# Weight sums of three pairs made by adding transfers, the root sent through DRAM, and four leading units kept in SBUF, at the entrance to the second ffn

## The chip, the cores and the metric

The kernel runs on one core of one Trainium2 chip. The metric is the device time of one execution in microseconds (us), less is better. A comparison is made from the medians of several runs; the profile is one further execution, with its own time.

Five engines matter: TensorE (PE for its matmuls, PEld for its weight loads), VectorE (DVE), ScalarE (ACT), GpSimd (POOL), and SyncE (SP), which here only issues transfers. POOL issues transfers too, on a queue of its own; those that add into their destination all go there.

## The reference

One decoder layer for 512 prompt tokens and 8 decode tokens (520 columns in all), float32, model width 1024, ffn width 2816:

```python
x = x + 0.5 * rmsnorm(swiglu(rmsnorm(x, ffn1_pre_g), ffn1_w_gate, ffn1_w_up, ffn1_w_down), ffn1_post_g)
m, ... = token_mixer(rmsnorm(x, mix_pre_g), ...)
x = x + rmsnorm(m, mix_post_g)
x = x + 0.5 * rmsnorm(swiglu(rmsnorm(x, ffn2_pre_g), ffn2_w_gate, ffn2_w_up, ffn2_w_down), ffn2_post_g)
```

with `swiglu(x) = (silu(x @ w_gate) * (x @ w_up)) @ w_down`. The token mixer runs a retention and a gated delta-rule branch side by side and ends in `y = sigmoid(gate_r) * (o_r @ w_ret_branch) + sigmoid(gate_g) * (o_g @ w_gdn_branch)`, then `y @ w_out`. The change lies between the end of that sum `y` and the first third of the second ffn.

## The kernel before, in words

**Layout.** Activations lie transposed: 8 tiles of 128 features by 520 tokens, in two halves of 260 columns (`HALVES`). A float32 product is made of three matmuls in the fast float32 format (`passes`, lines 414 to 416): high part of the weight by high part of the activation, high by low, low by high. So each weight tile is split first: ACT makes the high part (line 355, or 373 for half tiles) and DVE the low part (356, 374).

**Order of the work.** One Python program writes the instructions of all engines in one order. `tick` (line 223) is its clock: the loops that emit matmuls call it once per step of six matmuls, and it runs the side tasks (generators) that are due. A task that says `yield 4` goes on four steps later. Each engine carries out its own instructions strictly in the order written; an engine whose next instruction waits holds up all that are written behind it. The same holds for the transfers queued on SP and on POOL. `LATER` shifts single tasks by hand.

**Weights.** `unit_list` is the list of weight units in order of use. SP loads the raw unit of 512 KB into a ring of two buffers (`load_to`, lines 276 and 287), so a load waits until the split of the unit two before it is done. Splits run some units ahead (`prefetch`, line 312), unless `hold` is set, or, for pair units, `hold_sums`.

**Pairs.** In the second ffn the hidden tiles 0 to 3 are plain: 4 gate and 4 up products of 8 steps each. From tile 4 on, gate and up of a tile form a "pair": a 2 by 2 block product made with seven half-size products instead of eight (`SEVEN`, line 143; `product7`, line 843; tile name `sv` in the profile). With the blocks a11, a12 (gate) and a21, a22 (up), the seven weights are a11, a12, a22 and the sums s1 = a21 + a22, s3 = a11 + a21, s2 = a11 + a21 + a22 (with a sign) and s4 = a12 + a11 + a21 + a22. `begin_pair` (291) loads a first term of s1 and s3 and the whole a22 from SP; `add_sums` (304) then issues two adding transfers from POOL (line 307), each 256 KB. s2 and s4 are made on DVE when their turn comes (369 and 377). The token sides of the seven products are made by `token_factors` (801) on ACT and DVE; their high and low parts on 824 and 825.

**The end of the mixer.** `mixer` (1151) runs eight products of the first branch, then eight of the second (lines 1250 to 1259). `branch` (1262) evacuates each: for the second branch DVE forms gate times product (1281), POOL adds the first branch's part (1282), and three steps later ACT and DVE split the sum (1287, 1288) for the product with w_out, which `down` makes: five outputs one by one, and the last three with the first halves of all ahead of the second halves (`staged`). At its third output `down` loads x back (743, eight loads of 260 KB on SP). When a half is complete, `post` (629) takes the sum of squares over partitions by matmul (477), the inverse root on POOL (471, from `root`), spreads it over partitions by matmul (483, from `spread`) and adds the scaled output to x on POOL (647).

**The entrance to the second ffn.** `first_units` (765) runs the four leading units (gate and up of tiles 0 and 1) first over the first half of the tokens, then over the second. The first halves' four results are copied by ACT into two SBUF tiles "early" (792); the second halves' stay in their PSUM banks, of which there are eight. Meanwhile `pre_rms` (539) sums the squares of x, and `inverse_rms` (555) takes the root; four steps later it spreads each half by matmuls into a PSUM bank of its own and copies it to SBUF, one half by ACT (573), one by DVE (571). `hidden` (882) needs these two halves r[0], r[1] before it can use the leading units' results (889, 896). `token_factors` begins when the root instruction has been issued (`rooted`), and first issues the loads of the first two pairs (`begin_pairs`, 797). `hold_sums` is set from the start of `post` until r is there. `keep` (1072) stores x to DRAM once r is there.

Of the kernel before, what the change touches and what calls it, by code (L numbers as in the profile page):

```python
# [15 lines left out]
P = 128  # L16
# [14 lines left out]
HALVES = ((0, HC), (HC, HC))  # L31
BRANCH_HALVES = ((0, 256), (256, TOK - 256))
PIECES, PW = 3, -(-HC // 3)
PIECE_AT = [i * (HC - PW) // (PIECES - 1) for i in range(PIECES)]
KH = KD // 2
PAD = CONV_W - 1
TURN = 48
# [5 lines left out]
PLAIN = {1: 3, 2: 4}  # L43
SPLIT_H = (8, 21)
LEAD = 3
GATE_COLS = 72


# [122 lines left out]
class Kernel:  # L171
    def __init__(self, ctx, tc, a):
        self.tc, self.nc, self.a = tc, tc.nc, a
        nc = tc.nc
        pool = lambda name, **kw: ctx.enter_context(tc.tile_pool(name=name, **kw))
        self.cpool = pool("const", bufs=1)
        self.big = pool("big", bufs=SLOTS)
        self.raw = pool("raw", bufs=RAW_BUFS)
        self.whl = pool("whl", bufs=SPLIT_BUFS)
        self.wk = pool("wk", bufs=2)  # L180
        self.sm = pool("small", bufs=8)
        self.ps = pool("ps", bufs=8, space=PSUM)
        self.dram = pool("scratch", bufs=1, space=DRAM)
        self.n = 0
        self.unit_list = units()
        self.group, g, pairs = [], -1, {}
        for u in self.unit_list:
            if u[0] not in ("seven", "down7"):
                g += 1
                self.group.append(g)  # L190
                continue
            if u[0:3] not in pairs:
                g += 1
                pairs[u[0:3]] = g
            self.group.append(pairs[u[0:3]])
        self.group.append(g + 1)
        self.first_of = {}
        for j, g in enumerate(self.group):
            self.first_of.setdefault(g, j)
        self.loaded, self.begun = {}, {}  # L200
        self.split_done = {}
        self.raw_next = self.split_next = self.use_next = 0
        self.slots_used = 0
        self.freed = []
        self.sums_due = []
        self.hold_sums, self.pairs_upto = False, 0
        self.rooted = False
        self.ahead = 0
        self.tasks = []
        self.spawned = {}  # L210
        self.hold = False
        self.leads = 0
        self.now = 0
# [53 lines left out]
    def load_to(self, j):  # L267

        nc, a = self.nc, self.a
        while self.raw_next < min(self.group[min(j, len(self.unit_list))] + RAW_BUFS, self.group[-1]):  # L270
            u = self.unit_list[self.first_of[self.raw_next]]
            if u[0] == "seven":
                w, m = a[f"gu{u[1]}"], u[2]
                s1, s3, a22 = self.begun.pop((u[1], m), None) or self.begin_pair(u[1], m)
                t = self.raw.tile([P, KD, P], F32, tag="raw", name=self.name("raw"))
                nc.sync.dma_start(out=t, in_=w[2 * m])
                t = [t[:, 0:KH], s3, None, a22, t[:, KH:KD], s1, None]
            elif u[0] == "down7":
                t = []
                for d in (u[2], u[2] + 1):  # L280
                    raw = self.raw.tile([P, KD, P], F32, tag="raw", name=self.name("raw"))
                    nc.sync.dma_start(out=raw, in_=a[f"dn{u[1]}"][d, :, 0:KD, :])
                    t += [raw[:, 0:KH], raw[:, KH:KD]]
            else:
                kind, m, k0, k1 = u
                t = self.raw.tile([P, k1 - k0, P], F32, tag="raw", name=self.name("raw"))
                nc.sync.dma_start(out=t, in_=a[kind][m, :, k0:k1, :])
            self.loaded[self.raw_next] = t
            self.raw_next += 1
# [68 lines left out]
    def split_seven(self, j):  # L358

        nc = self.nc  # L360
        self.load_to(j)
        i = self.unit_list[j][3]
        t = self.loaded[self.group[j]]
        if i:
            self.add_sums(self.group[j])
        s2, s4 = 2, 6
        if i == s2:
            t[s2] = self.slot("s2", (P, KH, P))
            nc.vector.scalar_tensor_tensor(out=t[s2], in0=t[5], scalar=-1.0, in1=t[0], op0=ALU.mult, op1=ALU.subtract)  # L369
        w = self.whl.tile([P, 2, KH, P], F32R, tag="w", name=self.name("w7"))  # L370
        self.split_done[j] = (w[:, 0], w[:, 1])
        self.started(j)
        nc.scalar.copy(w[:, 0], t[i])  # L373
        nc.vector.tensor_tensor(w[:, 1], t[i], w[:, 0].bitcast(F32), ALU.subtract)  # L374
        if i == 4:
            t[s4] = self.slot("s4", (P, KH, P))
            nc.vector.tensor_tensor(t[s4], t[4], t[s2], ALU.subtract)

# [176 lines left out]
    def inverse_rms(self, acc, r, plus, held=False):  # L555
        nc = self.nc
        ps = self.bank("ss")
        self.sums(ps, acc, 2 * PIECES)
        m, s = self.root(ps, 2 * PIECES, 1.0 / D)
        if plus is not None:  # L560
            nc.vector.tensor_scalar(plus[0:PW], m[0:PW], EPS, None, ALU.mult)
        self.rooted = True
        self.hold = held
        if held:
            self.hold_sums = False
        yield 4
        out = self.wk.tile([P, TOK], F32, tag="rb", name=self.name("rb"), bufs=1)
        for hf, (c0, n) in enumerate(HALVES):
            pb = self.spread(s[:, hf * PIECES : (hf + 1) * PIECES])
            if hf:  # L570
                nc.vector.tensor_copy(out[:, c0 : c0 + n], pb)
            else:
                nc.scalar.copy(out[:, c0 : c0 + n], pb)
                if held:
                    yield 1
        for hf, (c0, n) in enumerate(HALVES):
            r[hf] = out[:, c0 : c0 + n]
        self.hold_sums = False

    def post_last(self, pairs, acc, sq, hf, plus):  # L580
# [184 lines left out]
    def first_units(self, xs, name, groups):  # L765
# [1 line left out]

        n = sum(len(g) for g in groups)
        ws, banks = [None] * n, [[None, None] for _ in range(n)]
        early = [self.slot("early") for _ in range(n // 2)]  # L770
        for hf, (c0, cols) in enumerate(HALVES):
            for group in groups:
                ps = {}
# [11 lines left out]
                for j in group:  # L785
                    banks[j][hf] = ps[j]
                    if hf:
                        self.release()
                    else:
                        rows = slice(0, ws[j][0].shape[2])  # L790
                        banks[j][0] = early[j // 2][rows, j % 2 * HC : j % 2 * HC + cols]
                        self.nc.scalar.copy(banks[j][0], ps[j][rows])
                if hf:
                    self.leads += 1
        return banks
# [1 line left out]
    def begin_pairs(self, f):  # L797
        for m in range(PLAIN[f], PLAIN[f] + 2):
            self.begun[f, m] = self.begin_pair(f, m, 24 if f == 1 and m > PLAIN[f] else SUM_LAG)

    def token_factors(self, xs, r, gcol, F, f):

        nc = self.nc
        while len(xs[1]) < KD or f == 2 and not self.rooted:
            yield 0

        if f == 2:
            self.begin_pairs(f)
        tt, stt = nc.vector.tensor_tensor, nc.vector.scalar_tensor_tensor
        for k in range(KH):  # L810
            x11, x12, x21, x22 = (self.x_of(z, hf) for z in (k, k + KH) for hf in range(2))
# [6 lines left out]
            nc.scalar.activation(ta[:, 0], d[:, 1], AF.Copy, scale=g1)  # L818
            stt(out=tb[:, 0], in0=x11, scalar=g1, in1=ta[:, 1], op0=ALU.mult, op1=ALU.subtract)
            stt(out=tb[:, 1], in0=x21, scalar=g2, in1=tb[:, 0], op0=ALU.mult, op1=ALU.subtract)  # L820
            yield 1
            for t, names in ((ta, ("T1", "T3")), (tb, ("T2", "T4"))):
                hi, lo = self.slot("th", (P, 2, HC), F32R), self.slot("tl", (P, 2, HC), F32R)
# [327 lines left out]
    def mixer(self, xs, r, plus_next, x_from):  # L1151
# [95 lines left out]
        for g in (GR, GG):  # L1247
            for m in range(KD):
                project(g, m)
        for out, g in ((RG, GR), (GZ, GG)):  # L1250
            for m in range(0, KD, 2):
                while out not in done:
                    self.tick()
                ox = [[self.ohl[out, h, hf] for h in range(H)] for hf in range(2)]
                hi, lo = self.next_unit()
                for z in range(2):
                    ks = slice(z * H, (z + 1) * H)
                    ps = self.product([((hi[:, ks, :], lo[:, ks, :]), range(H))], ox, "br", z, BRANCH_HALVES)
                    self.spawn(self.branch(g, m + z, gate.pop((g, m + z)), ps, part, yx))
        return self.down(yx, (8,), self.vec[:, V_MPOST : V_MPOST + 8], V_G2PRE, 3, None, plus_next, x_from)  # L1260

    def branch(self, g, m, gate, ps, part, yx):
# [15 lines left out]
        for hf, (c0, n) in enumerate(BRANCH_HALVES):  # L1278
            cs = slice(c0, c0 + n)
            ts.append(whole[:, cs])  # L1280
            nc.vector.scalar_tensor_tensor(out=ts[hf], in0=gate[:, cs], scalar=1.0, in1=ps[hf], op0=ALU.add, op1=ALU.mult)
            nc.gpsimd.tensor_tensor(ts[hf], ts[hf], part[m][:, cs], ALU.add)  # L1282
        yield 3
        for hf, (c0, n) in enumerate(BRANCH_HALVES):
            cs = slice(c0, c0 + n)
            t = ts[hf]
# [749 lines left out]
```

## Time and profile before

| | us |
|---|---|
| three runs: median (lowest to highest) | 1190.89 (1189.58 to 1191.94) |
| the profiled execution, its own time | 1189.49 |
| its span, first to last instruction | 1187.7 |
| TensorE matmul busy in it | 1172.0 |
| VectorE busy | 907.3 |
| ScalarE busy | 602.6 |
| GpSimd busy | 265.2 |
| end of the last product of the second branch, start of the product with w_out | 768.25 |
| the root of `inverse_rms` on POOL | 844.78 |
| the first pair products ("sv") | about 870 |

Places below are given in us from the start of the span. A row of the timeline has start, duration, engine, line, operation, output<-inputs, shapes and count, and in brackets how long the engine had been idle and what ended that. A row of the groups has the count, the busy time and mean duration in ns, and the idle time before them. A row of the waits has the total, the number of waits and the longest. A row of the windows has, for each engine, busy time and count, then the granted clock, the mean busy share of the 16 DMA engines, and GB/s. A row of the DMA queues has packets, MB, and the time the packets took as a share of 16 engines over the window; a row of the DMA issues has the count, the KB of each, and the median time from issue to landing.

### The profile page before, as it was taken

The numbers are of one execution on the slowest core, as the hardware profiler recorded it, in microseconds if no ns is written. First come the engines' busy times: TensorE is split into PE (matmuls) and PEld (weight loads), VectorE is DVE, ScalarE is ACT, GpSimd is POOL, SyncE is SP. The second block draws the span as 40 slices with busy tenths as digits, with TensorE's granted clock in tenths as the row PEclk, the third lists the DMA queues.
The fourth block names the chain that finished last, engine by engine and source line by source line (L and its number), as shares of the span: only waits on it lengthen the run. The fifth ranks groups of instructions, "written<-read, shape, count | busy, mean of one in ns | idle before, by whom it ended". The sixth has DMA issues, their size and how long they took to land. (4 is left out here: it accounts for less than half of the span.)

```text
span 1187.7 us, 25427 instructions
## 1 busy us (share of the span) xinstructions
PE 1172.0 (99%) x9831; PEld 1161.0 (98%) x9831; DVE 907.3 (76%) x1935; ACT 602.6 (51%) x1378; POOL 265.2 (22%) x477
## 2 busy tenths in 40 slices
PE   9999999999999999999999999999999999999998
PEld 8999999999999999999999999999999999999997
DVE  7988888777558788887677777746888888867555
ACT  7656666544336456313354774335555666644331
POOL 1111111000005248755551101404211111000000
PEclk9999999999999999999999999999999999999999
DMA  8777775233342533322367653242677777332334
GB/s 264 186 196 188 183 176 142 70 114 87 109 174 62 179 92 107 105 83 74 111 193 224 225 197 125 76 157 89 178 217 191 185 187 183 103 97 67 98 113 148
DMA packets 79178, 170.90 MB, mean 144 GB/s; under 512 B 17040, under 2 KB 18992, under 8 KB 79056
## 3 DMA queue, kind: packets, MB, share of 16 engines
q1 hardware_dynamic: 66768, 144.98, 38.1%
q0 software_dynamic: 12288, 24.29, 11.9%
q8 instruction: 77, 1.26, 0.4%
q14 instruction: 45, 0.37, 0.1%
HBM read 157.37 MB, written 11.86 MB: 142 GB/s over the span
## 5 line engine op out<-in xcount | busy, mean ns | idle before, releaser
L414 PE MATMUL p<-xhl,whi 128*128 128x260 f32 (+1 forms) x784 | 231.1, 295 | 0.0
L415 PE MATMUL p<-xhl,whi 128*128 128x260 f32 (+1 forms) x784 | 221.3, 282 | 0.1
L416 PE MATMUL p<-xhl,wlo 128*128 128x260 f32 (+1 forms) x784 | 221.2, 282 | 0.0
L356 DVE TENSOR_TENSOR wlo<-raw,whi 128x1024 fp32r<-128x1024 f32 (+2 forms) x111 | 132.9, 1202 | 50.1 <-ACT whi L355 48.4
L414 PE MATMUL sv<-th,w 128*128 128x260 f32 x592 | 167.6, 283 | 1.8 <-ACT q L912 1.8
L415 PE MATMUL sv<-tl,w 128*128 128x260 f32 x592 | 167.1, 282 | 0.0
L416 PE MATMUL sv<-th,w 128*128 128x260 f32 x592 | 167.1, 282 | 0.0
L415 PEld LDWEIGHTS p<-xhl,whi 128*128 128x128 f32 (+1 forms) x784 | 147.2, 188 | 0.7 <-DVE xhl L518 0.7
L414 PEld LDWEIGHTS p<-xhl,whi 128*128 128x128 f32 (+1 forms) x784 | 146.9, 187 | 0.9 <-DVE qk L1562 0.2
L416 PEld LDWEIGHTS p<-xhl,wlo 128*128 128x128 f32 (+1 forms) x784 | 147.0, 187 | 0.0
L307 POOL DMA_DIRECT2D s<-gu_in x74 | 65.0, 954 | 308.4 <-DMA s<-gu_in 156.1
L374 DVE TENSOR_TENSOR w<-s,w 128x512 fp32r<-128x512 f32 x148 | 101.6, 689 | 37.6 <-ACT w L373 36.7
L414 PE MATMUL dn<-hh,whi 128*128 128x260 f32 x448 | 127.0, 283 | 0.0
L415 PE MATMUL dn<-hl,whi 128*128 128x260 f32 x448 | 126.7, 283 | 0.0
L416 PE MATMUL dn<-hh,wlo 128*128 128x260 f32 x448 | 126.6, 283 | 0.0
L355 ACT CAST whi<-raw 128x1024 fp32r<-128x1024 f32 (+2 forms) x111 | 111.0, 1008 | 30.7 <-DMA raw<-dn_in 16.2
L414 PEld LDWEIGHTS sv<-th,w 128*128 128x128 f32 x592 | 111.3, 188 | 2.4 <-ACT q L912 2.2
L415 PEld LDWEIGHTS sv<-tl,w 128*128 128x128 f32 x592 | 111.5, 188 | 0.0
L416 PEld LDWEIGHTS sv<-th,w 128*128 128x128 f32 x592 | 111.4, 188 | 0.0
L373 ACT CAST w<-s 128x512 fp32r<-128x512 f32 x148 | 91.3, 618 | 34.1 <-DVE s L369 23.6
L471 POOL TENSOR_TENSOR rs<-ms,mhalf 87x3 f32<-87x3 f32 (+1 forms) x9 | 11.5, 1281 | 371.2 <-DVE ms L469 309.2
L416 PEld LDWEIGHTS dn<-hh,wlo 128*128 128x128 f32 x448 | 84.4, 188 | 0.0
(436 smaller groups left out, 3444.3 us busy)
## 6 DMA issues: line engine op xcount, KB each, us to landing
raw<-win_in SPq DMA_DIRECT2D x49, 512.0 KB, 3.6
raw<-gu_in SPq DMA_DIRECT2D x48, 512.0 KB, 5.2
s<-gu_in SPq DMA_DIRECT2D x74, 256.0 KB, 5.7
s<-gu_in POOLq DMA_DIRECT2D x74, 256.0 KB, 5.3
raw<-dn_in SPq DMA_DIRECT2D x32, 448.0 KB, 3.4
a<-gu_in SPq DMA_DIRECT2D x37, 256.0 KB, 5.8
x<-x SPq DMA_DIRECT2D x32, 260.0 KB, 5.5
raw<-dn_in SPq DMA_DIRECT2D x16, 512.0 KB, 3.6
```

The lines of the kernel that those rows point to most:

```text
L307: self.nc.gpsimd.dma_start(out=out, in_=term, accum_op=ALU.add)
L355: self.nc.scalar.copy(hi[:, ks], t[:, ks])
L356: self.nc.vector.tensor_tensor(lo[:, ks], t[:, ks], hi[:, ks].bitcast(F32), ALU.subtract)
L373: nc.scalar.copy(w[:, 0], t[i])
L374: nc.vector.tensor_tensor(w[:, 1], t[i], w[:, 0].bitcast(F32), ALU.subtract)
L414: mm(ps, hi[:, k, :], xh, start=first, stop=False, skip_group_check=more)
L415: mm(ps, hi[:, k, :], xl, start=False, stop=False, skip_group_check=more)
L416: mm(ps, lo[:, k, :], xh, start=False, stop=last, skip_group_check=more)
L471: self.nc.gpsimd.tensor_tensor(r[0:PW], m[0:PW], self.mhalf[0:PW].to_broadcast([PW, n]), ALU.pow)
```

## The change: what it does

1. **Whole pairs.** For the first three pairs of the second ffn (`WHOLE = 3`) all four sums s1, s2, s3, s4 are made by transfers. A new task `whole_pairs` is started after the first branch's products; six steps apart it issues per pair five plain loads of 256 KB from SP (`begin_whole`). Once the last product of the second branch has been written (`joined`), it issues 21 adding transfers of 256 KB from POOL, one per step: twelve that depend on nothing but the plain loads, then six and then three that add into a tile which an earlier one of them has written. `split_seven` makes no s2 and s4 on DVE for these pairs; the sign of s2 goes into its split. `begin_pairs` is no longer called for the second ffn.
2. **Root through DRAM.** For the second ffn `inverse_rms` hands over to `root_rows`: two steps after the root its 87 by 6 values are written to DRAM, three steps later four loads bring them back broadcast over all partitions, and six steps later r is set. The twelve spreading matmuls and the two copies of the spread root go away. The pieces are laid at columns 0, 87 and 173 instead of 0, 86 and 173, so that they follow each other in DRAM.
3. **Four units in SBUF.** In the second ffn the second halves' results of the leading units are copied to SBUF by ACT as well, and after each of the two groups one further weight unit is split.
4. **Earlier factors.** `token_factors` makes the first step's sums before the root and waits for it only then.
5. **Last branch sum.** The last of the eight adds of the second branch goes from POOL to DVE, and its split comes two steps later instead of three.

The diff, cut to its core:

```diff
-PIECE_AT = [i * (HC - PW) // (PIECES - 1) for i in range(PIECES)]
+PIECE_AT = [min(i * PW, HC - PW) for i in range(PIECES)]
+WHOLE = 3
...
@@ load_to
-                s1, s3, a22 = self.begun.pop((u[1], m), None) or self.begin_pair(u[1], m)
+                s1, s3, a22, *both = self.begun.pop((u[1], m), None) or self.begin_pair(u[1], m)
...
@@ split_seven
-        if i == s2:
+        if i == s2 and not whole:
...
+        if whole and i == s2:
+            nc.scalar.activation(w[:, 0], t[i], AF.Copy, scale=-1.0)
+            nc.vector.scalar_tensor_tensor(
+                out=w[:, 1], in0=t[i], scalar=-1.0, in1=w[:, 0].bitcast(F32), op0=ALU.mult, op1=ALU.subtract
+            )
...
-        if i == 4:
+        if i == 4 and not whole:
...
@@ inverse_rms
+        if plus is not None and not held:
+            yield from self.root_rows(s, r)
+            return
...
+    def root_rows(self, s, r):
+        nc = self.nc
+        n = PIECES * PW
+        yield 2
+        d = self.dram.tile([2 * n], F32, name=self.name("root"))
+        nc.sync.dma_start(out=d.rearrange("(c p) -> p c", p=PW), in_=s[0:PW])
+        yield 3
+        out = self.wk.tile([P, TOK], F32, tag="rb", name=self.name("rb"), bufs=1)
+        last = PIECE_AT[-1]
+        for hf, (c0, _) in enumerate(HALVES):
+            for at, to in ((0, last), (n - PW, HC)):
+                t0 = to - (PW if at else last)
+                nc.sync.dma_start(
+                    out=out[:, c0 + t0 : c0 + to], in_=d[hf * n + at : hf * n + at + to - t0].unsqueeze(0).to_broadcast([P, to - t0])
+                )
+        yield 6
+        for hf, (c0, cols) in enumerate(HALVES):
+            r[hf] = out[:, c0 : c0 + cols]
+        self.hold_sums = False
...
@@ first_units
+        both = name == "g"
...
+                if both and hf:
+                    self.prefetch(True, 1)
+                for j in group:
+                    if both or not hf:
...
+                        self.nc.scalar.copy(banks[j][hf], ps[j][rows])
...
+    def begin_whole(self, f, m, later):
+        dma, w = self.nc.sync.dma_start, self.a[f"gu{f}"]
+        s1, s3, a22, s2, s4 = (self.slot(x, (P, KH, P)) for x in ("s1", "s3", "a22", "s2", "s4"))
+        a11, a12, a21, a4 = (w[2 * m + i, :, k : k + KH] for i in range(2) for k in (0, KH))
+        for out, term in ((s3, a11), (s1, a21), (s2, a11), (s4, a12), (a22, a4)):
+            dma(out=out, in_=term)
+        for out, term in ((s3, a21), (s1, a4), (s2, a21), (s4, a11)):
+            later[0].append((out, term))
+        later[1] += [(s2, a4), (s4, a21)]
+        later[2].append((s4, a4))
+        self.begun[f, m] = s1, s3, a22, s2, s4
+
+    def whole_pairs(self, f):
+        later = [[], [], []]
+        for m in range(PLAIN[f], PLAIN[f] + WHOLE):
+            self.begin_whole(f, m, later)
+            yield 6
+        while not self.joined:
+            yield 0
+        for terms in later:
+            for out, term in terms:
+                self.nc.gpsimd.dma_start(out=out, in_=term, accum_op=ALU.add)
+                yield 1
+            yield 2
...
@@ token_factors
-        while len(xs[1]) < KD or f == 2 and not self.rooted:
+        while len(xs[1]) < KD:
             yield 0
-        if f == 2:
-            self.begin_pairs(f)
...
+            while f == 2 and not self.rooted:
+                yield 0
             yield 1
...
@@ mixer
+            if out == GZ:
+                self.spawn(self.whole_pairs(2))
...
+        self.joined = True
...
@@ branch
-            nc.gpsimd.tensor_tensor(ts[hf], ts[hf], part[m][:, cs], ALU.add)
-        yield 3
+            eng = nc.vector if m == KD - 1 else nc.gpsimd
+            eng.tensor_tensor(ts[hf], ts[hf], part[m][:, cs], ALU.add)
+        yield 3 if m < KD - 1 else 2
```

More of the change, by code (lines that the diff above doesn't have):

```diff
@@ L207, in __init__ @@
         self.rooted = False
+        self.joined = False
         self.ahead = 0
@@ L273, in load_to @@
                 w, m = a[f"gu{u[1]}"], u[2]
-                s1, s3, a22 = self.begun.pop((u[1], m), None) or self.begin_pair(u[1], m)
+                s1, s3, a22, *both = self.begun.pop((u[1], m), None) or self.begin_pair(u[1], m)
                 t = self.raw.tile([P, KD, P], F32, tag="raw", name=self.name("raw"))
                 nc.sync.dma_start(out=t, in_=w[2 * m])
-                t = [t[:, 0:KH], s3, None, a22, t[:, KH:KD], s1, None]
+                t = [t[:, 0:KH], s3, None, a22, t[:, KH:KD], s1, None, bool(both)]
+                if both:
+                    t[2], t[6] = both
             elif u[0] == "down7":
@@ L366, in split_seven @@
         s2, s4 = 2, 6
-        if i == s2:
+        whole = t[7]
+        if i == s2 and not whole:
             t[s2] = self.slot("s2", (P, KH, P))
@@ L372, in split_seven @@
         self.started(j)
-        nc.scalar.copy(w[:, 0], t[i])
-        nc.vector.tensor_tensor(w[:, 1], t[i], w[:, 0].bitcast(F32), ALU.subtract)
-        if i == 4:
+        if whole and i == s2:
[3 more added lines that the diff above has]
+            )
+        else:
+            nc.scalar.copy(w[:, 0], t[i])
+            nc.vector.tensor_tensor(w[:, 1], t[i], w[:, 0].bitcast(F32), ALU.subtract)
+        if i == 4 and not whole:
             t[s4] = self.slot("s4", (P, KH, P))
@@ L563, in inverse_rms @@
         self.hold = held
-        if held:
-            self.hold_sums = False
+        if plus is not None and not held:
+            yield from self.root_rows(s, r)
+            return
+        self.hold_sums = False
         yield 4
@@ L577, in inverse_rms @@
             r[hf] = out[:, c0 : c0 + n]
+        self.hold_sums = False
+    def root_rows(self, s, r):
[16 more added lines that the diff above has]
+            r[hf] = out[:, c0 : c0 + cols]
         self.hold_sums = False
@@ L769, in first_units @@
         ws, banks = [None] * n, [[None, None] for _ in range(n)]
-        early = [self.slot("early") for _ in range(n // 2)]
+        both = name == "g"
+        early = [[self.slot("early") for _ in range(n // 2)] for _ in range(1 + both)]
         for hf, (c0, cols) in enumerate(HALVES):
@@ L788, in first_units @@
                         self.release()
-                    else:
+                if both and hf:
+                    self.prefetch(True, 1)
+                for j in group:
+                    if both or not hf:
                         rows = slice(0, ws[j][0].shape[2])
-                        banks[j][0] = early[j // 2][rows, j % 2 * HC : j % 2 * HC + cols]
-                        self.nc.scalar.copy(banks[j][0], ps[j][rows])
+                        banks[j][hf] = early[hf][j // 2][rows, j % 2 * HC : j % 2 * HC + cols]
+                        self.nc.scalar.copy(banks[j][hf], ps[j][rows])
                 if hf:
```

## The prediction

> **What bounds the kernel now.** The page first: which engine fills the span.
>
> ```profile
> span 1187.7 us, 25427 instructions
> PE 1172.0 (99%) x9831; PEld 1161.0 (98%) x9831; DVE 907.3 (76%) x1935; ACT 602.6 (51%) x1378; POOL 265.2 (22%) x477
> ```
>
> TensorE is busy 99% of the span, and at full granted clock (the 1.00 in the windows below), so a change that leaves its matmuls alone can win only its idle spots and what matmuls it removes. The waits view of TensorE over 760 to 900, the stretch that the change touches, says where the idle spots are:
>
> ```profile
> PE dn L414 <- ACT yh L1287: 0.6, 1, 0.6
> PE u L414 <- ACT rb L573: 0.5, 1, 0.5
> PE sv L414 <- ACT q L912: 0.5, 1, 0.5
> PE g L416 <- DVE wlo L356: 0.5, 1, 0.5
> PE u L414 <- DVE h L896: 0.5, 1, 0.5
> PE ss L477 <- DVE acc L529: 0.4, 1, 0.4
> PE u L414 <- DVE rb L571: 0.4, 1, 0.4
> ```
>
> Seven waits, 3.4 us together. A wait costs more than its idle time, because matmuls overlap, as the timeline of TensorE shows:
>
> ```profile
> 754.75 0.28 PE L415 MATMUL br<-ol,whi 128*128 128x256 f32 x1
> 754.87 0.28 PE L416 MATMUL br<-oh,wlo 128*128 128x256 f32 x1
> 847.28 1.47 PE L483 MATMUL rb<-cst,rs 87*128 87x87 f32 x12
> 851.48 0.38 PE L414 MATMUL u<-xhl,whi 128*128 128x260 f32 x1 [0.53 <-ACT rb L573]
> ```
>
> One takes 0.28 us and the next starts 0.12 after it; a stop therefore loses its idle time plus 0.16. A step of six matmuls is 0.72 us. The third row is the spread of the root: 1.47 us of TensorE's own time, which the change deletes.
>
> **Gain 1: root and leading units.** The twelve matmuls leave: 1.47. The two waits on rb (0.5 and 0.4) are for the banks that the spread used; there is none any more: 0.9 + 2 x 0.16 = 1.2. The wait on h (L896) is for a bank that the leading units hold until they are used; with these in SBUF the four plain products after them need eight banks and find them: 0.5 + 0.16 = 0.66. The price is four copies by ACT, and the root comes by a longer way. Rows for both:
>
> ```profile
> L792 ACT COPY early<-g x4: 357/372/381, 823.5 to 832.5; 128x260 f32<-128x260 f32 x4
> 845.21 0.51 ACT L818 ACTIVATE ta<-xd,vec 128x260 f32<-128x260 f32 x1 [8.53 <-DVE xd L816]
> 844.48 0.16 DVE L467 TENSOR_SCALAR ms<-ss 87x6 f32<-87x6 f32 x1 [2.72 <-PE ss L477]
> 844.78 1.58 POOL L471 TENSOR_TENSOR rs<-ms,mhalf 87x6 f32<-87x6 f32 x1 [10.50 <-DVE ms L467]
> s<-pack SPq DMA_DIRECT2D x32, 8.0 KB, 2.7
> rb<-rrow SPq DMA_DIRECT2D x16, 256.0 KB, 5.5
> ```
>
> Four more copies are 4 x 0.37 = 1.5 us, and ACT idles 8.5 us there: nothing, while that idle time lasts; without it they would delay the factors by 1.5. The root is done at 846.4. No row has a transfer of 4-byte pieces; I bound the write by the small stores, 2.7, and by the broadcast loads, 5.5, and the loads back by the same two: r lands between 851.8 and 857.4. The program sets r eleven steps after the sums, which DVE reads at 844.48: 844.5 + 7.9 = 852.4. Until then DVE has the factor work, all of which is now written ahead of `hidden`, so a late r meets a busy DVE; I take 0. SP stands still for the first landing, and behind it are loads of pair weights whose splits `hold_sums` keeps back until r anyway. That flag falls seven steps (5 us) later than before, which leaves 17 us until the first pair products at about 870.
>
> [...]
>
> **Gain 2: sums off DVE.** In the groups and windows:
>
> ```profile
> L369 DVE SCALAR_TENSOR_TENSOR s<-s,raw 128x512 f32<-128x512 f32 x2 | 1.4, 684 | 0.0
> L377 DVE TENSOR_TENSOR s<-raw,s 128x512 f32<-128x512 f32 x1 | 0.7, 686 | 0.0
> 842.00:862.00 20.00, 19.11 (x162) 18.70 (x161) 16.44 (x33) 11.36 (x21) 5.16 (x5) 1.00 0.93 266
> 862.00:882.00 20.00, 19.02 (x155) 18.48 (x154) 18.05 (x37) 12.09 (x26) 3.48 (x4) 1.00 0.83 238
> ```
>
> The groups are those of 842 to 876. DVE (third pair of figures in a window) is 82% and 90% busy. Three sums leave up to 876, 2.1 us; the first step of the factors moves into DVE's 2.7 us of idle time ahead of L467; two weight splits come earlier. That is enough for the wait on q (0.5 + 0.16 = 0.66), which is a copy queued on ACT behind a split that waits for s2. Were DVE not relieved in time, the 0.66 would stay.
>
> **Gain 3: last branch sum.**
>
> ```profile
> 768.32 2.44 POOL L1282 TENSOR_TENSOR bt<-bt,yr 128x256 f32<-128x256 f32 x2 [1.33 <-DVE bt L1281]
> 772.09 1.44 POOL L1282 TENSOR_TENSOR bt<-bt,yr 128x256 f32<-128x256 f32 x2 [1.33 <-DVE bt L1281]
> 771.60 0.75 DVE L1281 SCALAR_TENSOR_TENSOR bt<-gate,br 128x256 f32<-128x256 f32 x2
> ```
>
> The last pair of adds ends at 773.53. On DVE the two products and two adds take turns: 771.60 + 4 x 0.37 = 773.1. So 0.4 earlier. The earlier products and POOL's lag stay.
>
> Gains: 1.47 + 1.2 + 0.66 + 0.66 + 0.4 = 4.4 us; I take 4.3. The waits on wlo and acc, around 821 to 825, are not touched.
>
> **The price: 21 adding transfers.** They are queued on POOL from 770.8, when its adds for the seventh product end (768.32 + 2.44), and share the 16 DMA engines with w_out and x. Rows: queue totals of the window 844 to 862 and of the whole run, the windows, x loads without and with adds beside them, and POOL's next work.
>
> ```profile
> q0 software_dynamic: 576, 1.05, 32.7%
> q0 software_dynamic: 12288, 24.29, 11.9%
> 745.00:772.00 27.00, 27.00 (x228) 27.00 (x228) 20.42 (x36) 8.73 (x17) 14.12 (x14) 1.00 0.27 83
> 772.00:812.00 40.00, 39.30 (x328) 38.89 (x328) 19.02 (x38) 12.71 (x23) 2.72 (x4) 1.00 0.41 143
> 850.00:860.00 10.00, 9.11 (x73) 8.70 (x73) 9.09 (x21) 6.97 (x15) 1.26 (x2) 1.00 1.06 274
> x<-x SPq DMA_DIRECT2D x8, 260.0 KB, 5.1
> x<-x SPq DMA_DIRECT2D x6, 260.0 KB, 10.0
> L307 POOL DMA_DIRECT2D s<-gu_in x74 | 65.0, 954 | 308.4 <-DMA s<-gu_in 156.1
> 809.16 0.86 POOL L471 TENSOR_TENSOR rs<-ms,mhalf 87x3 f32<-87x3 f32 x1 [35.62 <-DVE ms L467]
> ```
>
> Four adds took 0.327 x 18 = 5.9 us of all engines, 1.47 each (1.53 by the whole run). The L307 row shows that POOL stands still until a tile's earlier transfer has landed. The last add needs the landing of the 18th, and behind it on POOL waits the root at 809.16, for which TensorE, next, waits with its spread of the first half. So 18 x 1.47 = 26.5 us must be through, beside 0.41 x 40 = 16.4 us of other loads (143 GB/s x 40 = 5.7 MB, so 2.88 us per MB). Of those, two of the three loads of leading units slip out of the stretch, since their buffers come free later: 2 x 0.52 MB, 3.0 us. The first add's packets start at 772, and the engines reach a share of 1.06 when pressed: (26.5 + 16.4 - 3.0) / 1.06 = 37.6, so 809.6. One more issue (0.95) and the root starts at 810.6, where 809.16 - 0.4 = 808.8 would be due: 1.8 us lost. Bounds: 0 if the adds are through by 808, and 8.1 in the slow rival below. I take 1.8, since the 844 to 862 stretch is the nearest in mixture.
>
> The fifteen plain loads, 3.9 MB and 11.3 us of the engines, go out between 745 and 772, where these are busy for 0.27 x 27 = 7.3 us, and are needed only from 770 on: 0. The splits of these pairs cost what they did.
>
> **Sum.** 4.3 - 1.8 = 2.5 us. The profiled execution, 1189.49 (span 1187.7 and 1.8 around it), would become 1187.0; it lies 1.4 below the median of the runs, 1190.89, so the median becomes 1188.4. About 0.2% (2.4 us) is what a measurement of this kernel can tell from no change; the forecast lies on that border.
>
> **Rivals.**
>
> *The weights arrive late (same).* x is loaded while the adds run; issued from 778.41 on. Eight x loads (0.266 MB each, 0.77 us) against eight adds, turn by turn, take 8 x (1.47 + 0.77) / 1.06 = 16.9 us, to about 796; the raw unit of the seventh w_out tile, issued at 784.01 and behind them in SP's queue, shares its own 1.5 us with one more add, 2.8, and lands at 799 to 801.2 (an estimate).
>
> ```profile
> 778.41 3.75 SPq L743 DMA_DIRECT2D x<-x  x8
> 784.01 6.01 SPq L287 DMA_DIRECT2D raw<-wo_in  x2
> 792.93 1.04 ACT L355 CAST whi<-raw 128x1024 fp32r<-128x1024 f32 x1
> 801.27 0.39 ACT L528 ACTIVATE s<-dn 128x260 f32<-128x260 f32 x1 [1.55 <-PE dn L416]
> L356 DVE TENSOR_TENSOR wlo<-raw,whi 128x1024 fp32r<-128x1024 f32 x3 | 3.6, 1222 | 0.3 <-ACT whi L355 0.2
> ```
>
> Its split runs at 792.93 now and its product starts when the one evacuated at 801.27 ends, 0.4 sooner after the change. Landed at 801.2, split by 1.04 + 1.22, the low part is there at 803.5: 2.6 lost, in which the wait for the root hides. Then 4.3 - 2.6 = 1.7: 1189.2. For it: x loads beside adds took 10.0 instead of 5.1. Against: 4.9 us more than the few that a unit now takes would still be in time for 800.9.
> [...]
>
> *POOL is held past the root (slower).* At 1.53 per add, a share of 1.0 and no load slipping, 18 adds and the loads take 27.5 + 16.4 = 43.9: 815.9, and the root starts at 816.9, 8.1 late. 4.3 - 8.1: 3.8 slower, 1194.7. It decides from a root later than 813.1. For it: adds have never run in such a row in this trace. Against: the loads that slip.
>
> *The relief doesn't come (same).* If r or the factors still arrive late, the waits on q, h and the like move elsewhere, and only 1.47 + 0.4 is won: against 1.8, nothing; 1190.8. The idle time of ACT and DVE speaks against it.
>
> **Chances.** Forecast 0.44, late weights 0.22, POOL held 0.24, no relief 0.10. The forecast's own range is 1186.6 (adds for nothing, 4.3) to 1190; I give four fifths of it to faster by over 0.2%, 0.35, and 0.03 of the late weights' lucky end: 0.38. Slower takes most of the held POOL, 0.22; 0.40 remains for no change. The range runs from 1186.4 to 1194.0, which leaves out the worst of the held POOL and little below.
>
> **What would show it.** In the new profile: no rb matmuls near 847 and no TensorE wait on rb, h or q between 843 and 876; the first pair products about 4 us closer to the end of the leading units; adds on POOL from 771 and the last issued near 810; TensorE waiting on POOL's root at the first-half spread by 1 to 2 us. Wrong: a TensorE wait of 3 us or more there (POOL held), or on wlo or whi near 801 (late weights), or DVE still over 90% busy with waits behind it after 850 (no relief).

## The result, and the profile after

The changed kernel takes 1200.93 us (median of 4 runs, 1200.28 to 1201.88), the kernel before 1191.41 beside it: ratio 1.0083, 95% interval 1.0065 to 1.0100. It is 0.8% slower. The forecast was 1188.4, in a range to 1194.0; the result lies outside it. The profiled execution took 1200.4, 10.9 more than the one of before.

The head of the page, then the waits of TensorE over 760 to 900 (total, count, longest):

```profile
span 1198.6 us, 25432 instructions
PE 1175.4 (98%) x9819; PEld 1164.2 (97%) x9819; DVE 904.6 (75%) x1930; ACT 604.6 (50%) x1381; POOL 276.6 (23%) x490
```

```profile
PE dn L425 <- ACT whi L359: 5.7, 1, 5.7
PE sv L425 <- DVE t L953: 3.2, 1, 3.2
PE g L427 <- DVE wlo L360: 1.1, 2, 0.6
PE dn L427 <- DVE wlo L360: 0.5, 1, 0.5
PE ss L488 <- DVE acc L540: 0.4, 1, 0.4
PE dn L425 <- ACT yh L1355: 0.2, 1, 0.2
```

The waits on rb, h and q are gone, as forecast, and the one on yh fell from 0.6 to 0.2. Two new ones stand on top. And TensorE is busy for 3.4 us more, with twelve matmuls fewer: something made its matmuls longer.

**The first stop**, in the timeline (brackets: idle time before, and what ended it):

```profile
805.79 1.04 ACT L359 CAST whi<-raw 128x1024 fp32r<-128x1024 f32 x1 [12.77 <-DMA raw<-wo_in]
806.87 1.23 DVE L360 TENSOR_TENSOR wlo<-raw,whi 128x1024 fp32r<-128x1024 f32 x1 [12.62 <-ACT whi L359]
806.89 0.59 PE L425 MATMUL dn<-yh,whi 128*128 128x260 f32 x1 [5.70 <-ACT whi L359]
808.15 0.59 PE L427 MATMUL dn<-yh,wlo 128*128 128x260 f32 x1 [0.46 <-DVE wlo L360]
```

ACT had stood idle for 12.8 us until the raw unit of the seventh w_out tile landed. The split of that unit ran at 792.93 before; now it runs at 805.79. This is the place that the prediction named for its rival of the late weights, not the root on POOL, which started at 818.4 behind TensorE's own delay.

Why the unit was late: the DMA queues and issues of two windows, 778 to 788 and 788 to 806 (q0: the adding transfers; q1: all that SP issues), and SP's issues.

```profile
q0 software_dynamic: 863, 1.57, 85.9%
q1 hardware_dynamic: 334, 0.89, 24.8%
x<-x SPq DMA_DIRECT2D x8, 260.0 KB, 15.1
raw<-wo_in SPq DMA_DIRECT2D x1, 512.0 KB, 8.1
```

```profile
q0 software_dynamic: 1205, 2.19, 65.8%
q1 hardware_dynamic: 1210, 2.72, 43.7%
raw<-wo_in SPq DMA_DIRECT2D x2, 512.0 KB, 17.4
```

```profile
778.45 8.07 SPq L777 DMA_DIRECT2D x<-x  x8
788.21 3.35 SPq L291 DMA_DIRECT2D raw<-wo_in  x2
```

Up to 788 the adds sent 863 packets against 334. Nine of them were queued before the first load of x, and at first they had the engines to themselves, as the queues of 774 to 782 show (SP's queue, q1, has no row there):

```profile
q0 software_dynamic: 794, 1.46, 108.6%
```

SP had issued the sixth w_out unit at 778.01. By the trace's packet records its first packet started at 782.24; before, that of the same unit started 1.0 us after the issue. It landed after 8.1 us, and behind it, from 784.86 to 802.61, came the packets of x. From 788 to 806 the two queues went packet for packet, 1205 to 1210, at a share of about 1.1 of the engines. So the seventh unit, issued at 788.21, had to wait for the x in front of it on its own queue, and for as many packets of adds: its packets began at 800.97, and it landed after 17.6 us, at 805.77, where such a unit took 3.7 before (the median of 778 to 806). SP needed 8.07 us for its eight issues of x instead of 3.75, 2.7 of them for the sixth unit's landing, and so issued the seventh unit later than before; that cost nothing more, since x was in front of it until 802 in any case. Why the sixth unit sent nothing for 4.2 us is not shown.

**The second stop.** POOL's root, SP, DVE, TensorE:

```profile
854.84 1.33 POOL L482 TENSOR_TENSOR rs<-ms,mhalf 87x6 f32<-87x6 f32 x1 [11.21 <-DVE ms L478]
```

```profile
858.70 0.33 SPq L278 DMA_DIRECT2D raw<-gu_in  x1
859.08 0.35 SPq L599 DMA_DIRECT2D root<-rs  x1
867.02 1.76 SPq L606 DMA_DIRECT2D rb<-root  x4
```

```profile
870.22 0.70 DVE L889 TENSOR_TENSOR tl<-tb,th 128x520 fp32r<-128x520 f32 x1
873.13 0.98 DVE L953 TENSOR_TENSOR t<-early,rb 128x260 f32<-128x260 f32 x2 [2.21 <-DMA rb<-root]
```

```profile
880.11 0.36 PE L425 MATMUL sv<-xhl,w 128*128 128x260 f32 x1 [3.17 <-DVE t L953]
```

The root is done at 856.17. SP issues the write 2.9 us later, behind a load that waits for its buffer; the 2 KB take 7.6 us until SP may go on; the last load lands at 873.59. That is 17.4 us after the root; before, the second copy of the spread root ended 6.0 us after it (846.36):

```profile
851.98 0.42 DVE L571 COPY rb<-rb 128x260 f32<-128x260 f32 x1
```

After the change DVE is not busy when r lands but has been idle for 2.21, with all of `hidden` still to do for TensorE's next bank.

**The half clock.** Windows in the first stop, behind it, and behind the second (the figure after the five engines is the granted clock):

```profile
802.00:806.00 4.00, 0.00 (x0) 0.00 (x0) 0.00 (x0) 0.20 (x1) 0.08 (x1) 1.00 1.07 303
808.00:810.00 2.00, 1.85 (x8) 1.85 (x9) 2.00 (x6) 1.33 (x2) 0.86 (x1) 0.50 1.10 195
882.00:884.00 2.00, 2.00 (x11) 2.00 (x11) 2.00 (x5) 1.69 (x4) 0.00 (x0) 0.50 1.00 361
```

The clock record is at 0.50 for 6.83 us from 806.41 and for 3.41 from 881.51. Matmuls then start 0.217 apart (809.18, 809.40, 809.62) instead of 0.12, so each such us loses 0.45. Before, the clock was 1.00 through this whole stretch.

By the first starts of TensorE's tiles the loss adds up so:

| stretch | before | after | difference |
|---|---|---|---|
| span's start to w_out ("dn") | 768.2 | 768.6 | +0.4 |
| w_out to the sums of the first half ("ss") | 40.0 | 48.9 | +8.9 |
| to the sums for the root | 35.2 | 36.1 | +0.9 |
| to the first pair ("sv") | 26.8 | 26.6 | -0.2 |
| to the second ffn's down products | 182.3 | 183.4 | +1.1 |
| from there to the last matmul | 130.0 | 130.3 | +0.3 |

The first stop accounts for its row: 5.70 and 0.46 idle with 0.16 for each are 6.5; of the 6.83 at half clock some 5.9 fall on running matmuls, and 5.9 x 0.45 = 2.7. Together they are 9.2, where the row has 8.9. In the fourth row the gain of about 3.5 is eaten by a stop of 3.17 + 0.16.

The third row is a wait that was not there before, on the low part of a weight, 0.57 + 0.16:

```profile
852.96 0.39 PE L427 MATMUL g<-xhl,wlo 128*128 128x260 f32 x1 [0.57 <-DVE wlo L360]
```

```profile
844.81 0.42 DVE L878 TENSOR_TENSOR xd<-x,x 128x260 f32<-128x260 f32 x1
851.69 2.35 DVE L360 TENSOR_TENSOR wlo<-raw,whi 128x1024 fp32r<-128x1024 f32 x2
```

The first step's factor sums (item 4 of the change) now run on DVE at 844.81, ahead of seven additions for the root and of this split. All twelve kernels below keep item 4, and all have a wait of 0.5 to 1.2 us in this place. That item 4 is its cause is read from the order on DVE; no run leaves it out.

### The profile page after: what moved, and what is told of

The parts are those of the page before. It is cut to its first block, busy times and chain, and to the rows that moved or that the text cites. A ratio compares the mean times of both kernels' runs of the same rounds, so it can differ in the third digit from the quotient of the medians.

```text
span 1198.6 us, 25432 instructions
## 1 busy us (share of the span) xinstructions
PE 1175.4 (98%) x9819; PEld 1164.2 (97%) x9819; DVE 904.6 (75%) x1930; ACT 604.6 (50%) x1381; POOL 276.6 (23%) x490
## 5 line engine op out<-in xcount | busy, mean ns | idle before, releaser
L311 POOL DMA_DIRECT2D s<-gu_in x68 | 59.2, 957 | 315.6 <-DMA s<-gu_in 136.6
L482 POOL TENSOR_TENSOR rs<-ms,mhalf 87x3 f32<-87x3 f32 (+1 forms) x9 | 11.3, 1257 | 345.3 <-DVE ms L480 308.4
L425 PEld LDWEIGHTS dn<-hh,whi 128*128 128x128 f32 x448 | 84.4, 188 | 0.0
```

The lines of the kernel that those rows point to most:

```text
L311: self.nc.gpsimd.dma_start(out=out, in_=term, accum_op=ALU.add)
L425: mm(ps, hi[:, k, :], xh, start=first, stop=False, skip_group_check=more)
L482: self.nc.gpsimd.tensor_tensor(r[0:PW], m[0:PW], self.mhalf[0:PW].to_broadcast([PW, n]), ALU.pow)
```

## The experiments

**Theory L**: the adding transfers crowd x and the last w_out units out of the DMA engines, which makes the first stop. **Theory R**: the way through DRAM is long by itself and makes the second. Rivals: the order in which SP issues x; SP being held; the shift of the whole stretch by the first stop. Twelve kernels were run, each beside the kernel before; ratios are to that kernel.

**Each part undone, and both.** Without the whole pairs the pairs' transfers start at the root, as before; without the way through DRAM the root is spread by TensorE.

```diff
-WHOLE = 3
+WHOLE = 0
...
+            if f == 2 and not k:
+                for m in range(PLAIN[f] + WHOLE, PLAIN[f] + 2):
+                    self.begun[f, m] = self.begin_pair(f, m)
```

```diff
-        if plus is not None and not held:
-            yield from self.root_rows(s, r)
-            return
-        self.hold_sums = False
+        if held:
+            self.hold_sums = False
```

The first edit alone:

> The changed kernel without whole pairs (no plain loads ahead, no 21 adds; the first two pairs begun when the root is issued, as before), all else as changed. Theory L (the adds make the seventh w_out unit late): the wait of TensorE on ACT's split near 806, 5.7 us idle and the half clock after it, goes; the time falls by about 9 to 1192, and the wait before the first pair product stays at about 3 us. Rival to L (the order of x ahead of the weights in SP's queue alone is at fault): the wait near 806 stays and the time is about 1201.

The second alone:

> The changed kernel with the root spread by matmuls as before, whole pairs kept. Theory R (the root through DRAM is late, not VectorE's load): the 3.2 us wait before the first pair product goes with its half clock (1.7), the twelve matmuls come back (1.5): about 1197.5; the wait near 806 stays. Rival to R (VectorE is behind in any case): the wait stays, about 1202.4.

Both:

> The changed kernel without whole pairs and with the root by matmuls: the four units in SBUF, the earlier factors and the last branch sum on VectorE remain. If L and R are the two causes and each of the rest does as foretold: the wait on h gone (0.7), the branch wait 0.3 shorter, the spread's 1.5 kept: 1190 to 1190.5 against 1191.4 of the kernel before. If a third cause lies in what remains, the time is over 1193.

Measured: 1200.21 (ratio 1.0072, 1.0054 to 1.0090), 1196.13 (1.0043, 1.0026 to 1.0060), 1190.73 (0.9993, 0.9983 to 1.0002). TensorE's top wait without the whole pairs, then without the way through DRAM:

```profile
PE sv L425 <- DVE t L956: 10.7, 1, 10.7
```

```profile
PE dn L425 <- ACT whi L359: 5.7, 1, 5.7
```

Each part brings its own stop. Without the whole pairs the first is gone; without the way through DRAM, and with the whole pairs, the second is. With neither part a wait of 1.6 us on t is left in the place of the second, without a half clock behind it:

```profile
PE sv L425 <- DVE t L954: 1.6, 1, 1.6
```

The first kernel missed its expected time by 8 us, because with the pairs' transfers beginning at the root the way through DRAM is longer still: r lands 22.9 us after the root (847.40 to 870.30), and TensorE runs at half clock for 13.65 us from 871.3. The rest of the change alone (units in SBUF, earlier factors, last branch sum) makes no difference that can be measured: the waits on rb and h are gone, and this one and the one on the low part have come.

**x loaded later**, at the fifth output of w_out instead of the third:

```diff
-            if d == 2 and x_from is not None:
+            if d == 4 and x_from is not None:
```

> The changed kernel with the eight x loads issued two outputs later, behind the last w_out units in SP's queue; 21 adds kept. If the units are late because they stand behind x, which takes turns with the adds: the seventh unit lands before 795, the wait near 806 goes, about 1192. If the adds' volume alone makes any load late: the unit still lands after 799 and the time is over 1196. If x itself then comes too late for the adds into x: a new wait of POOL on x near 812.

Measured: 1203.87 (1.0102, 1.0082 to 1.0121). The eighth w_out unit lands at 797.30 and the wait near 806 is gone, but the jam moves to the loads of the leading units: ACT waits 12.04 us for one of them, and its next evacuation, which stands behind that split, comes late.

```profile
PE ss L488 <- DVE acc L540: 8.7, 1, 8.7
```

Neither branch of the expectation came: the order decides which load is late, but another order does not help. The 21 adds take their 31 us of the DMA engines (21 x 1.47, by the price that the prediction worked out) from whatever is next.

**Adds written four steps apart**, root by TensorE:

```diff
-                yield 1
-            yield 2
+                yield 4
```

> The changed kernel with the root spread by TensorE as before, and its 21 adding transfers issued one every four steps (about 2.9 us) instead of one every step, so that they run from 771 to about 832. If the wait near 806 comes from the adds crowding x and the last w_out units out of the DMA engines (theory L), there is no wait over 1 us near 806 and no half clock, and the time is that of the same kernel with adds at once, 1196.1, less 5.7 of idle time and 3.4 of half clock: 1187.0, 4 to 5 us under the kernel before. If any adds among these loads hurt (the total is the limit, not the crowding), the loads of the leading units are late instead and it stays over 1193.

Measured: 1195.23 (1.0032, 1.0021 to 1.0043), beside 1196.13 at full pace. But the edit did not spread the adds. A step is a place in the program, not a time, and between these places POOL had nothing to wait for:

```profile
770.27 10.62 POOL L859 DMA_DIRECT2D s<-gu_in  x12
816.26 0.91 POOL L859 DMA_DIRECT2D s<-gu_in  x1
```

Fourteen adds were still issued from 770.27 to 783.37, the first of them some 0.6 us apart, as at full pace. The last seven came behind POOL's next work, the root of the first half at 813.06, from 816.26 on. So this kernel shows 14 adds ahead of the units and seven later: the seventh unit lands at 801.18 instead of 805.24, the long stop becomes a shorter one of 1.8 + 0.8, and among the leading units the wait on the low part that all kernels have grows to 1.2 and one on xhl comes (the last two rows), with 3.41 at half clock twice. That fits theory L. An even spread was not measured, and neither branch of the expectation is tested by this run.

```profile
PE dn L425 <- ACT whi L359: 1.8, 1, 1.8
PE dn L427 <- DVE wlo L360: 0.8, 1, 0.8
PE g L427 <- DVE wlo L360: 1.7, 2, 1.2
PE g L426 <- DVE xhl L529: 0.6, 1, 0.6
```

**The clock kept up** by 48 further matmuls in the idle time of the first stop:

```diff
+                if fill and not hf and j == 1 and s == 0:
+                    spare, before = self.dbank("fill", n), steps[0][0][0]
+                    for _ in range(fill):
+                        self.nc.tensor.matmul(spare, before[0][:, 0, :], xs[hf][0][0], start=True, stop=True)
```

> The changed kernel with 48 more matmuls, into a bank that nobody reads, in the idle time ahead of the seventh w_out product, so that TensorE does not stand still there. If the 6.8 us at half clock after that wait come from TensorE's standing still, they go and the time falls by 3.4 us, to about 1197.5, though the weights land no earlier; if the half clock comes from something else, it stays, and the time is 1200.9 or above.

Measured: 1204.01 (1.0100, 1.0080 to 1.0121). Windows of this kernel, in the filled stretch and behind it:

```profile
803.00:808.00 5.00, 5.00 (x44) 5.00 (x43) 0.00 (x0) 0.49 (x1) 0.72 (x2) 1.00 1.08 299
810.00:812.00 2.00, 2.00 (x17) 2.00 (x18) 2.00 (x5) 1.33 (x2) 0.47 (x1) 1.00 1.11 207
```

The half clock near 806 is gone, so it does come from TensorE's standing still. But the time did not fall. From the arrival of the high part to the sums it takes 9.9 us (808.6 to 818.5) instead of 10.6 (806.9 to 817.5): of the 2.7 us only 0.7 come back. TensorE now waits there for DVE instead, 0.75 for the low part (0.46 without the further matmuls) and 1.42 for the sum of squares; DVE is busy for 2.00 of 2.00 us in the row above. The rest of the loss lies at the second stop: r came 19.7 us after the root here instead of 17.4, the wait on t grew from 3.2 to 5.5 and the half clock behind it from 3.41 to 6.83. Why the way through DRAM took 2.3 us longer in this kernel was not followed.

**The root's write on POOL's queue**, straight behind the root, so that SP's load is not in front of it:

```diff
-        nc.sync.dma_start(out=d.rearrange("(c p) -> p c", p=PW), in_=s[0:PW])
+        nc.gpsimd.dma_start(out=d.rearrange("(c p) -> p c", p=PW), in_=s[0:PW])
```

> The changed kernel with the write of the root issued by POOL, behind the root that POOL computes, instead of by SP behind a load of pair weights. If SP's being held (856.2 to 859.1) and the raw load ahead of it in the same queue make up the lateness, r lands 3 to 5 us earlier, the wait of 3.2 us on t and the half clock of 3.4 us behind it go, and the time is about 1196 (1200.9 less 3.2 and 1.7). If the write in itself is slow, r lands at most 2 us earlier and the time is 1199 or more.

Measured: 1200.84 (1.0076, 1.0057 to 1.0094), no change. DMA issues of this kernel, 858 to 872 (last figure: from issue to landing):

```profile
rb<-root SPq DMA_DIRECT2D x2, 86.5 KB, 5.8
rb<-root SPq DMA_DIRECT2D x2, 43.5 KB, 6.6
root<-rs POOLq DMA_DIRECT2D x1, 2.0 KB, 9.2
```

The write takes 9.2 from POOL, the loads back 5.8 to 6.6: r comes 18.3 us after the root. So SP's being held is not what makes r late, since the write issued without it takes longer still; the two transfers in a row are.

**Fewer adds**, root by TensorE: one whole pair (7 adds), then two (14).

```diff
-WHOLE = 3
+WHOLE = 1
```

> One pair's sums by seven adding transfers instead of three pairs' by 21, the second pair's transfers begun at the root as before, and the root spread by TensorE. Seven adds of 1.5 us are through by about 783, so theory L expects no wait near 806 and no half clock: 1188 to 1190, between the kernel with neither part (1190.7) and the gains of all three pairs (about 1187). If even a few adds delay the last w_out units, a wait of 1 us or more stays near 806 and the time is 1191 or more.

> Two pairs' sums by 14 adding transfers, root spread by TensorE. With 7 adds the eighth w_out unit landed at 796.8, with 21 at 808.4; if the landing goes with the number of adds (theory L), it lands near 802.6 here, the product waits 1 to 3 us, and the time is 1190 to 1193, above the kernel with one pair (1189.25). If the wait has a threshold between 14 and 21 (x and the units through before the second and third level of adds), there is no wait, one more pair's sums are off VectorE, and the time is 1188 to 1189.

Measured: 1189.25 (0.9978, 0.9968 to 0.9988) and 1192.62 (1.0011, 1.0002 to 1.0020). Median from issue to landing of the w_out units in the window 778 to 806 with one pair, then with two:

```profile
raw<-wo_in SPq DMA_DIRECT2D x3, 512.0 KB, 6.0
```

```profile
raw<-wo_in SPq DMA_DIRECT2D x3, 512.0 KB, 12.0
```

The eighth unit lands at 792.81 without adds (the kernel with neither part) and at 796.75, 804.28 and 807.91 with 7, 14 and 21, always with the root by TensorE. With 7 nothing waits for it. With 14 TensorE waits twice for 0.8 us, and a row at half clock follows:

```profile
804.40:807.40 3.00, 3.00 (x15) 3.00 (x15) 3.00 (x7) 1.24 (x2) 0.00 (x0) 0.50 0.64 169
```

**One pair, units left in their banks** (which also takes away the further splits of item 3):

```diff
-        both = name == "g"
+        both = False
```

> The kernel with one pair's sums ahead and the root spread by TensorE, but only the first half of the four leading units copied to SBUF, as in the kernel before. The prediction gave the copies of both halves 0.7 us by the wait on h and, with the waits for banks of the spread, up to 1.9 together. If that holds, the waits on rb and h of 0.4 to 0.5 us each come back and the time is 0.7 to 1.9 us above 1189.25, 1190 to 1191. If the copies do nothing, it is 1189.25 within 0.5 and the gain belongs to the sums alone.

Measured: 1189.07 (0.9979, 0.9969 to 0.9989). The waits on rb come back, and the time does not:

```profile
PE u L425 <- DVE rb L582: 0.4, 1, 0.4
PE u L425 <- ACT rb L584: 0.3, 1, 0.3
```

With these waits the first pair starts 1.2 us later than in the kernel with one pair, the down products only 0.6 later, and the difference of the medians is within their intervals.

**One pair, root through DRAM** (the kernel with one pair, without the second edit above):

> One pair's sums ahead as in the kernel at 1189.25, but the root through DRAM, so that the price of that way shows without a stop near 806. Theory R (a write of about 8 us, loads of 5 to 7 us behind it and among others, r some 17 us or more after the root) expects a wait of 3 to 8 us on t near 873, 3 to 14 us at half clock behind it, and 1194 to 1199. If the root was late only because the whole stretch had been shifted by the earlier stop, r lands within 11 us of the root and the time is 1190 or less.

Measured: 1193.56 (1.0020, 1.0011 to 1.0029), 4.3 above the same kernel with the root by TensorE (5.0 by the ratios). When `hidden` uses r first, by TensorE and then through DRAM:

```profile
854.89 0.76 DVE L954 TENSOR_TENSOR t<-early,rb 128x260 f32<-128x260 f32 x2
```

```profile
863.45 0.43 DVE L956 TENSOR_TENSOR t<-early,rb 128x260 f32<-128x260 f32 x1 [0.94 <-DMA rb<-root]
866.56 0.43 DVE L956 TENSOR_TENSOR t<-early,rb 128x260 f32<-128x260 f32 x1 [2.68 <-DMA rb<-root]
```

No earlier stop shifted anything here, and r still comes 18.7 us after the root. Theory R holds; the rival of the shift falls.

**Four of 14 adds before the last branch products**, root by TensorE:

```diff
+        for out, term in later[0][:4]:
+            self.nc.gpsimd.dma_start(out=out, in_=term, accum_op=ALU.add)
+            yield 2
+        del later[0][:4]
         while not self.joined:
```

> Two pairs' sums by adding transfers as in the kernel at 1192.6, but the first four of the 14 go out from about 755, between the branch sums on POOL, where the DMA engines are busy for 27% only, instead of from 771. Theory L: ten adds are left to compete with x and w_out, the eighth unit lands near 800 instead of 804.3, the waits of 0.8 and 0.8 near 803 and the half clock of 3.4 us behind them go, and the time is 1188 to 1189.5. Rival: the branch sums, which TensorE needs at 774, come behind the adds on POOL, the wait on yh there grows from 0.3 to over 1 us, and the time stays over 1190.

Measured: 1188.96 (0.9985, 0.9975 to 0.9995). The eighth unit lands at 798.17, and no wait on whi or wlo stands near 803 any more; the price is this row, 0.4 more than with all adds behind the branch:

```profile
PE dn L425 <- ACT yh L1360: 0.7, 1, 0.7
```

Against the same 14 adds at 1192.62 that is 3.7 us (3.1 by the ratios) for moving four of them to where the DMA engines had room (a share of 0.27 from 745 to 772 before). It is no faster than one pair alone.

## Why the prediction was wrong, point by point

- **Gain 3, last branch sum**: 0.4 forecast; the stop at 774 went from 0.62 to 0.25 us. Right.
- **Gains 1 and 2, waits on rb, h, q and the spread**: these waits went, and the stretch from the root's sums to the first pair would be some 3.5 us shorter without the new stop (-0.2 measured, 3.33 added back), where 1.47 + 1.2 + 0.66 = 3.3 were forecast. Right in that stretch; but the earlier factors, which were to use idle time of DVE, cost 0.9 in the stretch ahead of it. And the 1.2 for the waits on rb is worth 0.6 or nothing at the end (the kernel with units in their banks): the pairs behind were not bound by TensorE alone.
- **Price of the adds, 1.8**: the step that failed first. It was charged to the root on POOL. The adds did run as costed (last one issued at 809.03, "near 810"), but the charge fell on the w_out units. The rival *late weights* had the place and the mechanism, and the sign that the prediction gave for it (waits on wlo or whi near 801), at 2.6 us; it measured 8.9. Its sum let eight x loads take turns with eight adds from 778.41, for 16.9 us. That they take turns was the author's assumption, for which the prediction has no row. The turns were right: the packets of x ran for 17.7 us (784.86 to 802.61), and from 788 to 806, where both queues were full, the adds had 1205 packets and SP's queue 1210. The start was not: the sixth w_out unit, ahead of x in SP's queue, stood nowhere in the sum, and while nine adds were queued it sent its first packet at 782.24 and its last at 785.44, so x began at 784.86. The seventh unit landed 4.6 us beyond its later bound, and 2.7 at half clock came on top.
- **Root through DRAM, 0**: the step that failed second. "A late r meets a busy DVE; I take 0": DVE stood idle for 2.21, since everything that it still owed TensorE came after r in its order. r was bounded to 11.0 us after the root (857.4 - 846.4) and came 17.4 after it; the write took 7.6, where the rows taken for it had 2.7 and 5.5. Price: 4.3 with one pair, 4.8 with three (1200.93 - 1196.13), 9.5 with none (1200.21 - 1190.73).
- **The write of the root**, by the trace's packet records: its 4-byte packets start between 861.5 and 863.0, at 51 per 0.1 us from 862.0 to 862.6, so sending them costs about 1.4 us of the 7.6; the rest lies ahead of the first packet and behind the last.
- **POOL held** did not decide: the root on POOL never came behind an add. **Relief doesn't come** was wrong too: with one pair, 7 adds and the spread kept, 1.5 us less than with neither part, and 2.1 (0.22%) less than before.
- **The half clock** stood nowhere in the prediction; 1.00 in every row of before was taken as given.

Of the forecast gain, 4.3 - 1.47 - 1.2 = 1.6 does not hang on the root. The one-pair kernel measured 2.1 (1.4 to 3.8 by its interval), but not by these terms alone: its wait on q stayed at 0.4, the earlier factors cost 0.9, and leaving the units in their banks changed nothing.

## What to carry to other kernels

Before traffic is put into an idle stretch of the DMA engines, look up what is queued next and when it is needed: here the seventh unit stood behind x on its own queue while the two queues sent 1205 and 1210 packets from 788 to 806, and it landed after 17.6 us, where 3.7 was the median before. A hop through DRAM in the middle of a dependent chain came 11 to 17 us later than a spread by matmul here (17.4 and 22.9 us after the root, against 6.0 before), and it is hidden only if the engine behind it has that much work that doesn't need the result. To put transfers a number of steps apart in the program spreads them in time only if their engine waits in between: 14 of 21 adds written four steps apart went out in a row. Try one unit of such a change first: here one pair of three gave all the gain that was measured.

## What the runs showed of the hardware

- After the stop of 5.70 us TensorE's clock record was at one half for 6.83 us, and after the one of 3.17 for 3.41; over all kernels, the last microseconds of a run aside, half clocks of 3.41, 6.83, 10.24 and 13.65 were seen behind stops, multiples of 3.41. With 14 adds two waits of 0.8 us, 1.3 apart, had one behind them; in the kernel before, the single waits of 0.4 to 0.6 between 760 and 900 had none, and neither had the one of 1.6 in the kernel with neither part.
- The half clock near 806 cost less than its length times 0.45, with DVE close behind: 0.7 of 2.7 us came back when it was removed by the 48 further matmuls.
- Some half clocks stay unexplained: one of 3.41 us near 414 in eight of the twelve experiments, where TensorE has no stop, and one at 852 with the adds written four steps apart, behind a wait of 1.2 us. Single profiled spans carry some 1.5 us of this (3.41 x 0.45), which is why the verdicts above rest on the medians.
- A write of 522 values of 4 bytes held SP for 7.6 us in the changed kernel and for 11.3 among the first pairs' loads, in the one without the whole pairs; from POOL it took 9.2. In the changed kernel its last packet starts 3.9 us after the issue (859.08 to 862.98), and SP goes on 4.0 us after that, at 867.02.
